# The diagonal and the first neighbour level of a gated recurrence: matrix products before, elementwise products summed over rows by four wide matrix products after

## The chip, the cores and the metric

The kernel runs on one core of one Trainium2 chip. The metric is the device time of one execution in microseconds (us). TensorE (PE in the profile) multiplies matrices: it holds one 128x128 operand (its load is PEld) and streams the other, up to 512 columns, past it. VectorE (DVE), ScalarE (ACT) and GpSimd (POOL) do elementwise work, and SyncE (SP) issues transfers. Each engine takes its own instructions in a fixed order. An instruction that waits for another engine holds everything behind it on its own engine.

## The reference, cut to what matters

The kernel computes one layer of an encoder on 512 tokens of width 1024: attention beside a bidirectional gated recurrence, then attention into a memory, then a gated MLP. The change concerns the recurrence:

```python
def step(S, xs):
    qx, kx, vx, lx = xs
    bcum = jnp.cumsum(lx, axis=-2)
    diff = bcum[..., :, None, :] - bcum[..., None, :, :]
    dec = jnp.exp(jnp.where(tri, diff, -jnp.inf))
    a = jnp.einsum("...tk,...sk,...tsk->...ts", qx, kx, dec)
    o_intra = jnp.einsum("...ts,...sv->...tv", a, vx)
    ...
out = out[0] + flip(out[1])
```

For each of 4 heads this is an attention without softmax. The weight between positions t and s is a sum over 128 key channels of q at t, k at s and the product of the gates between them; k is one minus the gate. It runs forward and backward, and both results are added. So the diagonal (s = t) gets q times the sum of both k, and the pair of positions 2i and 2i+1 gets q times k times one gate.

## The kernel before, in words

Channels lie on the 128 partitions and the 512 tokens along a row. Most of the program is fp32 arithmetic from parts: each operand is split into a rounded part `hi` (type fp32r) and a rest `lo`, and `mm3` (lines 277 to 280) multiplies hi with hi, hi with lo and lo with hi. These wide products (128x512) are nearly all of TensorE's rows.

The recurrence is `hgrn_core(h)`, one call per head. It works by levels m = 1, 2, 4 to 256. At level m, q and k have been multiplied by the gates up to the edge of their block of m positions. A 128x128 product per block of 128 tokens then gives the weights between neighbouring blocks of m, and a mask picks them into `diag`. One level goes so: ScalarE copies the k side of level m into `kc` (line 644), TensorE multiplies four 128x128 blocks (line 647), VectorE multiplies the k side and then the q side by the gates of the next level (line 673, two instructions), multiplies pairs of gates (line 678) and puts the result into `diag` by mask (line 679). Ahead of that, `ksum` is the sum of both directions' k (lines 628 and 629), `kc` and `qc` are gathered (line 632), the product of `ksum` with `q` (line 636) gives the diagonal, and ScalarE copies it into `diag` (line 637). Level 1 uses `kc` and `qc`. These products take plain fp32 operands, in which the trace shows two records per 128x128 product.

`weave` interleaves streams of work. Three heads of the core run between the input projections (share 53 of 100), the fourth beside the attention. Each `yield` of a stream says how much was done. The framework then gives each engine a fixed order, by what it reckons to be ready. `mem_turn` (lines 803 to 806) transposes the memory rows (line 317) into the PSUM banks `ps_s` and `ps_o`, from which lines 121 and 122 split them on ScalarE and VectorE; each bank name has two buffers, and the next token projection (`put`s into `ps_s` and `ps_o`) needs them back. At the end of a head, ScalarE squares the output (line 691), GpSimd takes the power (lines 296 and 297), VectorE scales (line 697) and TensorE transposes (line 701). `put_f` (lines 603 to 607) makes the gates and gated q of a head.

Of the kernel before, what the change touches and what calls it, by code (L numbers as in the profile page):

```python
# [9 lines left out]
F32 = mybir.dt.float32  # L10
F32R = mybir.dt.float32r
BF16 = mybir.dt.bfloat16
U8 = mybir.dt.uint8
# [36 lines left out]
CORE_SHARE, ATT_LEAD = 53.0, 4.0  # L50
KEY_TURNS = {1: (0, 1), 2: (2, 3)}
# [38 lines left out]
def layer(tc, io, out):  # L90
# [17 lines left out]
    def bank(tag):  # L108
        return ps.tile([P, 512], F32, name="ps_" + tag, tag=tag)
# [172 lines left out]
    def blk(b):  # L282
        return slice(b * P, (b + 1) * P)
# [156 lines left out]
    ones = const.tile([P, P], F32, name="ones")  # L440
# [97 lines left out]
    masks = const.tile([P, len(LEVELS), P], U8, name="masks")  # L538
    masks_f = tmp4([P, len(LEVELS), P])
# [4 lines left out]
    with tc.issue_after(last_load[0]):  # L544
        nc.sync.dma_start(lbt, io["hg_lb"])
        nc.sync.dma_start(og, io["hg_out_norm_g"][:, None])
        nc.sync.dma_start(masks_f, io["masks"])
# [70 lines left out]
    def hgrn_core(h):  # L618
# [8 lines left out]
        ksum, kc, qc = [tmp2(tag="th") for _ in range(3)]  # L627
        nc.scalar.mul(ksum, qk[:, 1, 0, :], oml[:, 0, h:h + 1])
        nc.vector.scalar_tensor_tensor(out=ksum, in0=qk[:, 1, 1, :], scalar=oml[:, 1, h:h + 1], in1=ksum,
                                       op0=ALU.mult, op1=ALU.add)  # L630
        for side, to in ((1, kc), (0, qc)):
            (nc.vector.tensor_copy if (h, side) == (1, 0) else nc.scalar.copy)(
                to, pat(qk, side * 2 * T, [[2, T // 2], [T + 1, 2]]))
        o = bank("c").rearrange("p (b n) -> p b n", b=NB)
        for b in range(NB):
            nc.tensor.matmul(o[:, b, :], ksum[:, blk(b)], q[:, blk(b)], start=True, stop=True)
        nc.scalar.copy(diag, o)
        yield 1.0
        toff = 0
        for i, m in enumerate(LEVELS + (128, 256)):  # L640
            if m <= 64:
                if m > 1:
                    kc = tmp2(tag="th")
                    nc.scalar.copy(kc, pat(qk, 2 * T, [[2 * m, T // (2 * m)], [T + m, 2], [1, m]]))
                o = bank("c").rearrange("p (b n) -> p b n", b=NB)
                for b in range(NB):
                    nc.tensor.matmul(o[:, b, :], kc[:, blk(b)], qc[:, blk(b)] if m == 1 else  # L647
                                     pat(qk, b * P, [[2 * m, P // (2 * m)], [T + m, 2], [1, m]]),
                                     start=True, stop=True)
# [6 lines left out]
            else:  # L656
# [18 lines left out]
            if m < 128:  # L675
                src = tt[:, toff:toff + 2 * nblk].rearrange("p (i two) -> p two i", two=2)
                toff += 2 * nblk
                nc.vector.tensor_mul(tt[:, toff:toff + nblk], src[:, 0, :], src[:, 1, :])
                nc.vector.copy_predicated(diag, masks[:, i:i + 1, :].to_broadcast([P, NB, P]), o)
            else:  # L680
                nc.scalar.copy(a[:, :, 1, :], o)
            yield 1.0
# [664 lines left out]
```

## Time and profile before

| | |
|---|---|
| three timed runs | 815.26, 815.65, 817.07 us |
| median | 815.65 us |
| span of the profiled execution, first to last instruction | 813.8 us |
| what lies around the span, against the median | 1.85 us |
| granted TensorE clock, mean | 0.998 |
| heads 0 to 3 of the recurrence in the trace, first product of line 636 | 54.3, 99.5, 130.8, 195.4 us |

| stretch, us | PE busy | DVE busy | ACT busy |
|---|---|---|---|
| 50 to 76 (head 0) | 26.00 of 26 | 18.37 | 15.18 |
| 100 to 124 (head 1) | 23.28 of 24 | 19.73 | 12.83 |
| 124 to 160 (memory rows, head 2) | 35.92 of 36 | 24.97 | 21.84 |
| 160 to 194 (rotary queries) | 34.00 of 34 | 24.35 | 23.94 |
| 194 to 212 (keys, start of head 3) | 17.34 of 18 | 15.57 | 16.37 |

Busy time of TensorE is reckoned from modelled ends, so the trace's starts say more: the time from one start to the next is what a product costs the stream. In a row of the timeline the first number is the start, the second the busy time, both in us, then the engine, the line of the program, the operation, what it writes and reads, and how many instructions are merged. A bracket gives the idle time just before, and who ended it.

### The profile page before, as it was taken

What the parts mean: (1) busy time and instruction counts of PE and PEld (TensorE: products, weight loads), DVE (VectorE), ACT (ScalarE), POOL (GpSimd) and SP (SyncE); (2) the same over time, 40 slices, a digit from 0 to 9 for tenths busy, and PEclk for the clock granted to TensorE, in tenths of its full rate; (3) what the DMA queues carried; (4) which work ended last, traced back from release to release, by engine and by line L of the source; (5) the groups of instructions that cost most, each with busy time, mean ns of one, the idle gap of its engine ahead of it and who ended that gap; (6) DMA issues with size and microseconds to landing.
All of it is one profiled execution on the core that took longest, in us unless ns stands there. A gap on an engine that the chain in (4) does not pass through costs nothing.

```text
span 813.8 us, 11771 instructions
## 1 busy us (share of the span) xinstructions
PE 803.3 (99%) x4426; PEld 691.0 (85%) x4426; DVE 574.7 (71%) x868; ACT 482.1 (59%) x796; POOL 136.9 (17%) x213
## 2 busy tenths in 40 slices
PE   9999999999999999999999999999999999999996
PEld 7888888889998887888888898899999998888885
DVE  5456587469886865855453767987777788888765
ACT  5675757459988874644543553665555545566651
POOL 0111201053233102301010311211111111000301
PEclk9999999999999999999999999999999999999999
DMA  8685645569899753256634158776665677278852
GB/s 296 202 259 139 160 103 117 118 159 247 229 250 254 182 172 126 78 181 157 180 117 142 33 164 208 154 200 166 179 171 143 150 200 178 91 208 278 239 130 104
DMA packets 42457, 139.61 MB, mean 172 GB/s; under 512 B 5280, under 2 KB 6560, under 8 KB 42400
## 3 DMA queue, kind: packets, MB, share of 16 engines
q1 hardware_dynamic: 28944, 97.43, 35.5%
q0 software_dynamic: 12160, 38.54, 26.2%
q10 hardware_dynamic: 1296, 2.89, 1.0%
q8 instruction: 34, 0.56, 0.3%
q14 instruction: 23, 0.19, 0.1%
HBM read 135.17 MB, written 25.17 MB: 197 GB/s over the span
## 4 chain that ended last, share of the span: by engine, by line
PE 92%; DVE 3%; ACT 2%; issue 1%; POOL 1%; DMA 0%; DVEq 0%; POOLq 0%; SPq 0%; ACTq 0%
PE ps_b L279 10%; PE ps_b L280 10%; PE ps_b L278 10%; PE ps_s L278 6%; PE ps_s L280 6%; PE ps_s L279 6%; PE ps_o L278 5%; PE ps_o L279 5%; PE ps_o L280 5%; PE ps_c L278 5%; PE ps_c L280 5%; PE ps_c L279 5%; PE ps_c L647 3%; PE ps_o L893 2%; PE ps_s L872 2%; PE ps_o L882 2%
## 5 line engine op out<-in xcount | busy, mean ns | idle before, releaser
L222 ACT CAST wh<-raw 128x1024 fp32r<-128x1024 f32 x110 | 113.7, 1035 | 114.6 <-PE ps_b L279 35.3
L224 DVE TENSOR_TENSOR wl<-raw,wh 128x1024 fp32r<-128x1024 f32 (+1 forms) x77 | 92.3, 1201 | 72.2 <-ACT wh L222 72.0
L278 PE MATMUL ps_b<-big,wh 128*128 128x512 f32 (+1 forms) x344 | 122.3, 355 | 0.0
L280 PE MATMUL ps_b<-big,wl 128*128 128x512 f32 (+1 forms) x344 | 121.2, 352 | 0.0
L279 PE MATMUL ps_b<-big,wh 128*128 128x512 f32 (+1 forms) x344 | 121.2, 352 | 0.0
L280 PEld LDWEIGHTS ps_b<-big,wl 128*128 128x128 f32 x344 | 65.1, 189 | 8.5 <-DMA wl<-in_wu_dram 0.2
L278 PEld LDWEIGHTS ps_b<-big,wh 128*128 128x128 f32 x344 | 65.1, 189 | 8.3
L279 PEld LDWEIGHTS ps_b<-big,wh 128*128 128x128 f32 x344 | 65.1, 189 | 8.1
L673 DVE TENSOR_TENSOR big<-big 128x512 f32<-128x512 f32 x64 | 47.2, 755 | 9.6 <-PE ps_c L647 4.0
L278 PE MATMUL ps_s<-wh,big 128*128 128x512 f32 (+1 forms) x140 | 53.4, 383 | 0.0
L279 PE MATMUL ps_s<-wl,big 128*128 128x512 f32 (+1 forms) x140 | 53.3, 381 | 0.0
L280 PE MATMUL ps_s<-wh,big 128*128 128x512 f32 (+1 forms) x140 | 53.0, 379 | 0.0
L230 POOL DMA_DIRECT2D wl<-in_w_dram x33 | 29.3, 887 | 126.7 <-ACT wl L229 91.5
L122 DVE TENSOR_TENSOR big<-ps_o,big 128x512 fp32r<-128x512 f32 x54 | 36.9, 687 | 15.0 <-ACT big L121 13.4
L121 ACT CAST big<-ps_o 128x512 fp32r<-128x512 f32 x54 | 31.7, 588 | 18.5 <-PE ps_o L996 7.5
L278 PE MATMUL ps_s<-big,wh 128*128 128x256 f32 (+1 forms) x120 | 40.0, 334 | 0.0
L279 PE MATMUL ps_s<-big,wh 128*128 128x256 f32 (+1 forms) x120 | 40.0, 333 | 0.0
L280 PE MATMUL ps_s<-big,wl 128*128 128x256 f32 (+1 forms) x120 | 40.0, 333 | 0.0
L278 PE MATMUL ps_o<-wh,big 128*128 128x512 f32 (+1 forms) x102 | 39.2, 385 | 0.0
L279 PE MATMUL ps_c<-big,wh 128*128 128x256 f32 (+1 forms) x120 | 39.1, 326 | 0.0
L278 PE MATMUL ps_c<-big,wh 128*128 128x256 f32 (+1 forms) x120 | 39.1, 326 | 0.0
L280 PE MATMUL ps_c<-big,wl 128*128 128x256 f32 (+1 forms) x120 | 39.1, 326 | 0.0
(315 smaller groups left out, 2149.3 us busy)
## 6 DMA issues: line engine op xcount, KB each, us to landing
raw<-in_w_dram SPq DMA_DIRECT2D x91, 512.0 KB, 3.6
wl<-in_w_dram POOLq DMA_DIRECT2D x33, 512.0 KB, 7.3
sum_t<-in_wd_dram SPq DMA_DIRECT2D x20, 512.0 KB, 6.3
tmp<-in_wu_dram SPq DMA_DIRECT2D x14, 512.0 KB, 6.9
sum_t<-in_wd_dram POOLq DMA_DIRECT2D x10, 512.0 KB, 8.4
sum_t<-sum_t POOLq DMA_DIRECT2D x10, 512.0 KB, 7.5
big<-sum_t SPq DMA_DIRECT2D x10, 512.0 KB, 4.7
raw<-sum_t SPq DMA_DIRECT2D x10, 512.0 KB, 4.4
```

The costliest lines, as they stand in the source:

```text
L121: nc.scalar.copy(hi, src)
L122: (eng or nc.vector).tensor_sub(lo, src, hi.bitcast(F32))
L222: nc.scalar.copy(wh, raw)
L224: last_low[0] = nc.vector.tensor_sub(wl[:, :by_dma], raw[:, :by_dma], wh[:, :by_dma].bitcast(F32)).ins
L230: nc.gpsimd.dma_start(wl[:, by_dma:], source(i)[:, by_dma:], accum_op=ALU.add)
L278: nc.tensor.matmul(o, a[0], b[0], start=start, stop=False, skip_group_check=again)
L279: nc.tensor.matmul(o, a[0], b[1], start=False, stop=False, skip_group_check=again)
L280: last_mm[0] = nc.tensor.matmul(o, a[1], b[0], start=False, stop=stop, skip_group_check=again).ins
L647: nc.tensor.matmul(o[:, b, :], kc[:, blk(b)], qc[:, blk(b)] if m == 1 else pat(qk, b * P, [[2 * m, P // (2 * m)], [T + m, 2], [1, m]]), st ...
L673: nc.vector.tensor_tensor(out=c, in0=c, in1=pat(tt, toff + off, [[2, npair], [gap, 2], [0, m]]), op=ALU.mult)
L872: nc.tensor.matmul(s, qT[h // 4][:, h % 4, blk(qb)], kT[:, 2 * (h // 4) + c, :], start=c == 0, stop=c == 1)
L882: nc.tensor.transpose(o[:, c, :], e[:, 0, blk(c)], ident)
```

## The change

The diagonal and level 1 no longer go through 128x128 products of their own. VectorE forms the elementwise products of q and k for the diagonal and for the neighbouring position, in two instructions, into a tile `near` with two rows of 512: the first row holds, for each t, the term of the even s of t's pair, the second that of the odd s. ScalarE and VectorE split `near` into `hi` and `lo` (128x1024 each). TensorE sums over the 128 channels by multiplying with `parity`, a constant of alternating ones and zeros: with it shifted by one column for the second row, even output rows take the first row and odd ones the second. That is four 128x512 products per head. ScalarE copies the result into `diag`, whose other entries the masks of the later levels overwrite. The gather of `kc` and `qc` for level 1, its products and its mask are gone; the mask tile has 6 levels in place of 7. A `yield` of 1.5 (`PREP`) stands between the split and the four products, and the yield of 1.0 for level 1 is gone. `ones` moves from a constant to a temporary.

```diff
+PREP = 1.5
-    ones = const.tile([P, P], F32, name="ones")
+    parity = const.tile([P, P + 2], F32R, name="parity")
+    ones = tmp2((P, P), tag="tq")
     nc.gpsimd.memset(ones, 1.0)
+    for i in range(2):
+        nc.gpsimd.memset(parity.rearrange("p (i two) -> p i two", two=2)[:, :, i].bitcast(F32), 1.0 - i)
...
-        ksum, kc, qc = [tmp2(tag="th") for _ in range(3)]
+        near = room[:, 1024:2048]
+        ksum = tmp2(tag="th")
         nc.scalar.mul(ksum, qk[:, 1, 0, :], oml[:, 0, h:h + 1])
+        nc.vector.tensor_tensor(out=pat(near, T, [[2, T // 2], [1 - T, 2]]), in0=pat(qk, 0, [[2, T // 2], [T + 1, 2]]),
+                                in1=pat(qk, 3 * T + 1, [[2, T // 2], [-(T + 1), 2]]), op=ALU.mult)
         nc.vector.scalar_tensor_tensor(out=ksum, in0=qk[:, 1, 1, :], scalar=oml[:, 1, h:h + 1], in1=ksum,
                                        op0=ALU.mult, op1=ALU.add)
-        for side, to in ((1, kc), (0, qc)):
-            (nc.vector.tensor_copy if (h, side) == (1, 0) else nc.scalar.copy)(
-                to, pat(qk, side * 2 * T, [[2, T // 2], [T + 1, 2]]))
-        o = bank("c").rearrange("p (b n) -> p b n", b=NB)
-        for b in range(NB):
-            nc.tensor.matmul(o[:, b, :], ksum[:, blk(b)], q[:, blk(b)], start=True, stop=True)
-        nc.scalar.copy(diag, o)
+        pairs = lambda t: t.rearrange("p (i two) -> p i two", two=2)
+        nc.vector.tensor_tensor(out=pat(near, 0, [[2, T // 2], [T + 1, 2]]), in0=pairs(ksum), in1=pairs(q), op=ALU.mult)
+        hi, lo = [tmp4([P, 2, T], F32R) for _ in range(2)]
+        split(hi, lo, near.rearrange("p (a t) -> p a t", a=2))
+        yield PREP
+        o = bank("c")
+        for i in range(2):
+            for part in (hi, lo):
+                nc.tensor.matmul(o, parity[:, i:i + P], part[:, i], start=i == 0 and part is hi, stop=i == 1 and part is lo)
+        nc.scalar.copy(diag, o.rearrange("p (b n) -> p b n", b=NB))
         yield 1.0
...
-            if m <= 64:
-                if m > 1:
-                    kc = tmp2(tag="th")
-                    nc.scalar.copy(kc, pat(qk, 2 * T, [[2 * m, T // (2 * m)], [T + m, 2], [1, m]]))
+            if 1 < m <= 64:
+                kc = tmp2(tag="th")
+                nc.scalar.copy(kc, pat(qk, 2 * T, [[2 * m, T // (2 * m)], [T + m, 2], [1, m]]))
...
-                nc.vector.copy_predicated(diag, masks[:, i:i + 1, :].to_broadcast([P, NB, P]), o)
+                if m > 1:
+                    nc.vector.copy_predicated(diag, masks[:, i - 1:i, :].to_broadcast([P, NB, P]), o)
...
-            yield 1.0
+            if m > 1:
+                yield 1.0
```

The framework orders the engines anew. Three places matter below. Line numbers of the changed kernel are larger: its 278 to 280 are 279 to 281, 121 and 122 are 122 and 123, 126 is 127, 317 is 318, 577 is 581, 607 is 611, 647 is 656, 673 is 682, 678 is 687, 697 is 708, 701 is 712.

**TensorE in head 1, before.** In these rows `tmp2_733` is q, `tmp2_892` is `ksum`, and `ps_b_877` and `ps_b_1002` are two projections of head 2 of 24 wide products each.

```order
L278 MATMUL ps_b_877<-big_114,wh_737 128x512
L636 MATMUL ps_c_899<-tmp2_733,tmp2_892 128x128 x4
L279 MATMUL ps_b_877<-big_116,wh_737 128x512
L280 MATMUL ps_b_877<-big_114,wl_738 128x512
L278 MATMUL ps_b_877<-big_114,wh_737 128x512
L647 MATMUL ps_c_905<-tmp2_894,tmp2_893 128x128 x4
L279 MATMUL ps_b_877<-big_116,wh_737 128x512
L647 MATMUL ps_c_916<-big_731,tmp2_914 128x128 x4
L280 MATMUL ps_b_877<-big_114,wl_738 128x512
```

TensorE in head 1, after. `ps_b_876` and `ps_b_986` are the same two projections; `tmp4_896` is `hi`, `tmp4_897` is `lo`, and line 656 is level 2.

```order
L280 MATMUL ps_b_986<-big_118,wh_772 128x512
L281 MATMUL ps_b_986<-big_116,wl_773 128x512
L646 MATMUL ps_c_900<-tmp4_896,parity_86 128x512
L279 MATMUL ps_b_986<-big_116,wh_772 128x512
L656 MATMUL ps_c_911<-big_708,tmp2_909 128x128 x4
L646 MATMUL ps_c_900<-tmp4_897,parity_86 128x512
L646 MATMUL ps_c_900<-tmp4_896,parity_86 128x512
L646 MATMUL ps_c_900<-tmp4_897,parity_86 128x512
L280 MATMUL ps_b_986<-big_118,wh_772 128x512
```

The core's first product moved from within the first projection (13 wide products of it done) to the tenth place of the second (24 and 9 done). Level 2 now stands between the first and the second of the four summing products.

**TensorE where the memory rows are turned, before.** Ahead of these rows stand the last product of head 1's line 687 and 11 of 14 wide products of `ps_b_1082`. Line 317 turns the memory rows, line 701 the output of head 1 (`tmp2_1073`), and `ps_s_1163` is the first bank of the next token projection.

```order
L278 MATMUL ps_b_1082<-big_114,wh_823 128x512
L279 MATMUL ps_b_1082<-big_116,wh_823 128x512
L280 MATMUL ps_b_1082<-big_114,wl_824 128x512
L317 MATMUL ps_s_1122<-ident_84,big_454 128x128 x4
L317 MATMUL ps_o_1129<-ident_84,big_454 128x128 x4
L317 MATMUL ps_s_1136<-ident_84,big_454 128x128 x4
L317 MATMUL ps_o_1143<-ident_84,big_454 128x128 x4
L701 MATMUL ps_c_1184<-ident_84,tmp2_1073 128x128 x3
L278 MATMUL ps_s_1163<-wh_880,big_113 128x512
```

TensorE there, after. Line 698 is the old 687, 712 the old 701, and `ps_s_1158` is the first bank of the token projection.

```order
L697 MATMUL ps_c_1075<-big_325,big_890 128x128
L698 MATMUL ps_c_1075<-big_890,big_708 128x128
L281 MATMUL ps_b_1055<-big_117,wl_823 128x512
L318 MATMUL ps_s_1117<-ident_84,big_457 128x128 x4
L318 MATMUL ps_o_1124<-ident_84,big_457 128x128 x4
L318 MATMUL ps_s_1131<-ident_84,big_457 128x128 x4
L318 MATMUL ps_o_1138<-ident_84,big_457 128x128 x4
L712 MATMUL ps_c_1185<-ident_84,tmp2_1088 128x128 x4
L279 MATMUL ps_s_1158<-wh_879,big_116 128x512
```

Between the last product of head 1's core and the turning of the memory rows stood 14 wide products; now one does. The other 13 run earlier, between the levels of head 1.

**VectorE at the same place, after.** `tmp2_1109` is the last projection of head 2, line 708 the scaling of head 1's output, line 611 head 2's gated q, line 123 the rest of the split that gives `ps_s` and `ps_o` back.

```order
L581 TENSOR_TENSOR tmp2_1109<-ps_b_1055,big_301 128x512
L708 SCALAR_TENSOR_TENSOR tmp2_1088<-ps_c_1075,small_1094,big_657 128x128 x4
L611 SCALAR_TENSOR_TENSOR big_873<-big_874,oml_316,tmp2_875 128x512
L123 TENSOR_TENSOR big_1116<-ps_s_1117,big_1115 128x4x128
L123 TENSOR_TENSOR big_1116<-ps_o_1124,big_1115 128x4x128
```

VectorE there, before: `tmp2_1073` is the output of head 1, and line 122 gives `ps_s_1122` back.

```order
L697 SCALAR_TENSOR_TENSOR tmp2_1073<-ps_c_1060,small_1079,big_666 128x128 x4
L577 TENSOR_TENSOR tmp2_1114<-ps_b_1082,big_298 128x512
L122 TENSOR_TENSOR big_1121<-ps_s_1122,big_1120 128x4x128
L629 SCALAR_TENSOR_TENSOR tmp2_1192<-big_874,oml_313,tmp2_1192 128x512
L607 SCALAR_TENSOR_TENSOR big_874<-big_875,oml_313,tmp2_876 128x512
```

The release of the first `ps_s` bank now stands behind head 2's gated q (line 611) as well as behind the scaling of head 1.

More of the change, by code (lines that the diff above doesn't have):

```diff
@@ L536, in spread_r @@
             put_v(b, v_ps[b])
-    masks = const.tile([P, len(LEVELS), P], U8, name="masks")
-    masks_f = tmp4([P, len(LEVELS), P])
+    masks = const.tile([P, len(LEVELS) - 1, P], U8, name="masks")
+    masks_f = tmp4([P, len(LEVELS) - 1, P])
     lbt = const.tile([P, 2, 2, 4], F32, name="lbt")
@@ L546, in layer @@
         nc.sync.dma_start(og, io["hg_out_norm_g"][:, None])
-        nc.sync.dma_start(masks_f, io["masks"])
+        nc.sync.dma_start(masks_f, io["masks"][:, 1:, :])
         nc.sync.dma_start(qkg[:, 0, :], rows_bc(io["q_norm_g"], 64))
@@ L655, in hgrn_core @@
                                      start=True, stop=True)
-            else:
+            elif m == 256:
                 o = bank("c").rearrange("p (b n) -> p b n", b=NB)
```

2 lines of the change are left out of this document (1 added, 1 removed).

## The prediction

> **What bounds the kernel now.** I read the page's busy times first, then its chain of work that ended last, then TensorE's timeline in the four stretches in which a head of the recurrence runs.
>
> ```profile
> span 813.8 us, 11771 instructions
> PE 803.3 (99%) x4426; PEld 691.0 (85%) x4426; DVE 574.7 (71%) x868; ACT 482.1 (59%) x796; POOL 136.9 (17%) x213
> PE 92%; DVE 3%; ACT 2%; issue 1%; POOL 1%; DMA 0%; DVEq 0%; POOLq 0%; SPq 0%; ACTq 0%
> ```
>
> TensorE is busy for 803.3 of 813.8 us and makes 92% of the chain. So a product taken out of its stream is worth its whole length, and a wait put into it costs its whole length: its order is fixed, nothing overtakes. The median of the runs, 815.65 us, lies 1.85 above the span; I take those 1.85 as unchanged and reckon differences in the span.
>
> **What the products cost TensorE.** From the timeline of TensorE, head 0, and the groups by line:
>
> ```profile
> 54.08 0.39 PE L280 MATMUL ps_o<-wh,big 128*128 128x512 f32 x1
> 54.31 1.05 PE L636 MATMUL ps_c<-tmp,tmp 128*128 128x128 f32 x8
> 55.11 0.48 PE L278 MATMUL ps_o<-wh,big 128*128 128x512 f32 x1
> 55.43 1.05 PE L647 MATMUL ps_c<-tmp,tmp 128*128 128x128 f32 x8
> 56.24 0.48 PE L279 MATMUL ps_o<-wl,big 128*128 128x512 f32 x1
> ...
> 91.76 0.39 PE L278 MATMUL ps_b<-big,wh 128*128 128x512 f32 x1
> 99.24 0.39 PE L278 MATMUL ps_b<-big,wh 128*128 128x512 f32 x1
> ...
> L636 PE MATMUL ps_c<-tmp,tmp x32: 271/276/351, 54.3 to 196.2; 128*128 128x128 f32 x32
> L647 PE MATMUL ps_c<-tmp,tmp x32: 271/275/377, 55.4 to 200.0; 128*128 128x128 f32 x32
> ```
>
> Between 91.76 and 99.24 lie 33 wide products (7.48 us): 0.227 each. From 54.31 to 55.43 a group of line 636 and one wide product take 1.12, so the group costs 0.89, the slower start of the product behind it included. Removed are the groups of line 636 and of line 647 on `tmp`, 32 records each, 8 to a group: 8 groups, 7.12 us. Added are 16 wide products: 3.63 us. The trace has no row of a product with `parity`; its operands are fp32r like those of `mm3`, so I take 0.227. Bounds: 0.22 (the 0.89 of a plain fp32 group, spread over its 4 products) and 0.89 (plain fp32 over 512 columns). **Gain of TensorE's stream: 3.5 us**, 0.87 per head. It is the whole gain only if the new products find their operands ready.
>
> **Head 1: the longer way to the first product.** The chain here is VectorE's:
>
> ```profile
> 100.01 0.68 DVE L678 TENSOR_TENSOR big<-big 128x512 f32<-128x512 f32 x1
> 100.61 0.50 DVE L632 COPY tmp<-big 128x512 f32<-128x512 f32 x1
> 101.04 2.15 DVE L673 TENSOR_TENSOR big<-big 128x512 f32<-128x512 f32 x2
> 103.04 0.40 DVE L678 TENSOR_TENSOR big<-big 128x256 f32<-128x256 f32 x1
> 103.37 0.71 DVE L679 COPY_PREDICATED big<-masks,ps_c 128x512 f32<-128x512 uint8 x1
> 103.98 1.29 DVE L673 TENSOR_TENSOR big<-big 128x512 f32<-128x512 f32 x2
> ...
> 102.14 0.47 PE L279 MATMUL ps_b<-big,wh 128*128 128x512 f32 x1
> 103.33 1.20 PE L647 MATMUL ps_c<-big,tmp 128*128 128x128 f32 x8 [0.72 <-DVE big L673]
> ...
> L222 ACT CAST wh<-raw 128x1024 fp32r<-128x1024 f32 x110 | 113.7, 1035 | 114.6 <-PE ps_b L279 35.3
> L224 DVE TENSOR_TENSOR wl<-raw,wh 128x1024 fp32r<-128x1024 f32 (+1 forms) x77 | 92.3, 1201 | 72.2 <-ACT wh L222 72.0
> ```
>
> Level 2 came 1.19 after the wide product ahead of it, where 0.23 would do: a wait of 0.96, because line 673 at level 1 takes 1.0 for each side (101.04 to 103.04), at level 2 about 0.6. The two products into `near` (lines 634 and 639 of the changed kernel) are not in this trace. Line 634 reads and writes in the pattern of level 1: 1.0. Line 639 reads straight and writes in that pattern: 0.6 to 1.0; I take 0.8, the middle of its two nearest rows. hi is a cast of 128x1024 (1.0), lo a subtraction of that size (1.2).
>
> The Trainium skill, SBUF — State Buffer, section "Door 1: The DMA port swizzle", says that accesses keep full bandwidth when at least two in a row hit the same 16-byte line, and pay otherwise. The rows 101.04 and 103.98 agree (single elements 1.0, pairs 0.6). By that rule line 639, which writes single elements, would take 1.0, and the sum below would be some 0.4 us later.
>
> By the new order, on the clock of this trace: gate pairs until 100.61, line 634 until 101.6, gate pairs 0.33, line 639 until 102.7, two sides of level 1 until 104.7, gate pairs and a projection's line 581 until 105.5, lo until 106.7. ScalarE casts hi from 102.9 to 103.9, after a weight cast that waits for the end of the projection. TensorE comes to hi after 21 wide products from 99.24, at 104.0: no wait. Level 2 (104.5) waits for its q side until 104.8, and lo, 0.89 later, from 105.7 to 106.7. Together 1.3, with line 639 at its ends 1.1 to 1.5, for the 0.96 and some 0.1 at the group ahead of it that go: **+0.2, bounds 0 to +0.5**. In head 0 the same order leaves nine wide products (2 us) more before hi, and I find no wait.
>
> **Where the memory rows are turned.** Here the moved work counts. TensorE, ScalarE and VectorE before:
>
> ```profile
> 123.58 0.48 PE L279 MATMUL ps_b<-big,wh 128*128 128x512 f32 x1
> 126.88 0.60 PE L317 MATMUL ps_s<-ident,big 128*128 128x128 f32 x4
> 128.63 0.49 PE L701 MATMUL ps_c<-ident,tmp 128*128 128x128 f32 x3
> 129.16 0.50 PE L278 MATMUL ps_s<-wh,big 128*128 128x512 f32 x1
> ...
> 123.86 0.28 ACT L691 ACTIVATE tmp<-ps_c 128x128 f32<-128x128 f32 x1 [1.42 <-PE ps_c L687]
> 128.28 0.63 ACT L603 ACTIVATE big<-tmp 128x512 f32<-128x512 f32 x1
> 130.04 0.57 ACT L121 CAST big<-ps_o 128x512 fp32r<-128x512 f32 x1
> ...
> 126.44 1.13 DVE L697 SCALAR_TENSOR_TENSOR tmp<-ps_c,small,big 128x128 f32<-128x128 f32 x4 [3.21 <-POOL small L297]
> 127.49 0.68 DVE L577 TENSOR_TENSOR tmp<-ps_b,big 128x512 f32<-128x512 f32 x1
> 128.42 0.69 DVE L122 TENSOR_TENSOR big<-ps_s,big 128x512 fp32r<-128x512 f32 x1 [0.25 <-ACT big L121]
> 130.18 0.75 DVE L607 SCALAR_TENSOR_TENSOR big<-big,oml,tmp 128x512 f32<-128x512 f32 x1
> ```
>
> Let X be 123.58, when head 1's last product has left TensorE. ScalarE's squares, GpSimd's power and VectorE's scaling (line 697) take until X + 3.9. Before, 14 wide products and the turning covered that; the token projection at 129.16 started when line 122 had freed `ps_s`, 0.3 late. After, one wide product is left there. TensorE has that (0.31), the turning (126.88 to 128.63, 1.75) and four transposes (0.44): 2.5. `ps_s` comes free later: VectorE scales until X + 3.9, then does line 611 (0.7, for which ScalarE's lines 607 to 609 are ready in time: 1.76 as from 128.28 to 130.04, begun at about X + 1.3), then line 123 (0.7): X + 5.3. TensorE stands 2.8 for 0.3: **+2.5**. Bounds: 1.8 if line 611 cost nothing; 2.9 if the transposes, too, came only after the release.
>
> **Head 2.** The same queue leads on to head 2's `near`:
>
> ```profile
> 132.04 0.68 DVE L122 TENSOR_TENSOR big<-ps_o,big 128x512 fp32r<-128x512 f32 x1
> 132.79 0.43 DVE L715 TENSOR_TENSOR big<-big,qkg 128x256 f32<-128x256 f32 x1
> 134.14 0.69 DVE L678 TENSOR_TENSOR big<-big 128x512 f32<-128x512 f32 x1
> 134.74 0.75 DVE L126 SCALAR_TENSOR_TENSOR big<-ps_c,og,big 128x512 fp32r<-128x512 f32 x1
> 135.40 2.15 DVE L673 TENSOR_TENSOR big<-big 128x512 f32<-128x512 f32 x2
> ```
>
> From X + 5.2: three more splits (1.8), four rotary tables (1.35, from 132.79 to 134.14), line 634 (1.0), line 127 (0.66), `ksum` (0.66), one side (1.0), line 639 (0.8): X + 12.5. The cast makes hi at X + 13.5. TensorE reaches it 34 wide products after X + 5.3: X + 13.0, a wait of 0.5. lo is ready at X + 15.3 (one side 1.0, gates 0.6, lo 1.2), TensorE there at X + 14.6: 0.7. Together 1.2 for some 0.3 spread over head 2 before: **+0.9, bounds 0.5 to 1.2**.
>
> **Head 3** starts in the stretch of keys and attention. Before, level 2 waited there for ScalarE:
>
> ```profile
> 207.46 1.16 PE L647 MATMUL ps_c<-big,tmp 128*128 128x128 f32 x8 [0.52 <-ACT tmp L644]
> ```
>
> After, lo has to wait behind the first three keys in VectorE's order, and level 2 stands behind more projection work. That wait may go, stay, or be one like head 1's: **-0.2, bounds -0.5 to +1.0**. GpSimd's two fills of `parity` and SyncE's smaller mask transfer lie beside the first loads. VectorE's added work per head (1.0 + 0.8 + 1.2, less 0.6 for one mask) costs nothing where VectorE idles; if that cover were gone it would be 2.4 per head.
>
> **Sum.** -3.5 + 0.2 + 2.5 + 0.9 - 0.2 = -0.1, so 815.55: **815.5 us**. The change takes out what it says, and nearly all of it stands again as waits for VectorE. The terms' bounds add up to 814.0 and 817.8.
>
> **The rivals.** (a) *The waits are covered.* If the hole at the memory rows does not open (its work runs earlier than my walk has it), 2.5 comes back: 813.0. For it speaks that the chain before shows VectorE with only 3%; against it that the bank's release stands behind line 611 in the order. If head 1 and 2 run freely as well, 3.5 and the old 0.96 are gained: 811.2. (b) *VectorE bounds the start of the attention: slower.* In head 3, `near` and lo stand ahead of the last key in VectorE's queue. If the last key comes later than TensorE's turn of it, the attention starts late by up to the added 2.4, and with the upper ends of heads 1 and 2 (+0.6) it is 815.5 + 3.0 = 818.5. It decides from the point at which what is given back passes 3.5. Against it: level 1's two sides (2.0) moved behind the keys. (c) *The summing products do not run at 0.227* but at twice that, as two passes: 16 x 0.227 = 3.6 more, 819.1; at plain fp32's 0.89, 16 x 0.66 = 10.6 more, 826. Against it stand all rows of fp32r.
>
> **How the numbers follow.** A measurement of this kernel can tell about 0.2% (1.6 us) from no change: 814.0 to 817.3 is "same". My forecast's own range is 814.0 to 817.3, inside its bounds; it has 0.48. (a) has 0.32, all faster. (b) has 0.17 and (c) 0.03, all slower. The range for 8 in 10 reaches to 812.2 below, past (a)'s first value and to 818.0 above, past the sum of the upper bounds, to the lower half of (b).
>
> **What would show it.** In the changed profile: 16 products on `parity` at 0.23 from start to start; in head 1 a wait of about 1 ahead of the second of them, for VectorE's lo; TensorE idle for 2 to 3 us ahead of the first token projection into `ps_s`, ended by VectorE's line 123; in head 2 about half a microsecond ahead of the first and of the second summing product. The prediction is wrong if that idle time is under 1 us, or if the keys' transposes in head 3 wait for over 1 us.

## The result, and the profile after

| | before | after |
|---|---|---|
| median of the timed runs, us | 815.84 | 818.49 |
| runs, us | 815.26 to 817.30 | 817.48 to 821.37 |
| ratio of after to before, 95% interval | | 1.0033, 1.0023 to 1.0044 |
| span of the profiled execution, us | 813.8 | 816.8 |

The change made the kernel 0.33% slower; 815.5 had been forecast, and the range ended at 818.0. Of the experiments below, one execution of PREP 1.0 (1136 us) and one of PREP 1.0 with the seeds later (963 us) ran at granted clocks of 0.66 and 0.78: the ratios leave them out, the medians without them are 814.24 and 814.88 us, and the second was the profiled one, so its waits are left blank. On the page of the changed kernel, the span, the busy times and the chain of work that ended last:

```profile
span 816.8 us, 11680 instructions
PE 802.4 (98%) x4378; PEld 687.1 (84%) x4378; DVE 583.4 (71%) x875; ACT 481.7 (59%) x793; POOL 137.2 (17%) x215
...
PE 88%; DVE 6%; ACT 2%; DMA 2%; issue 1%; POOL 0%; DVEq 0%; POOLq 0%; SPq 0%
```

TensorE's share of the chain fell from 92 to 88%. VectorE has 6 for 3, and the DMAs, which had none, have 2. So TensorE waits more. Where, its timeline shows; a bracket holds the idle time ahead of the row and who ended it:

```profile
104.82 1.20 PE L656 MATMUL ps_c<-big,tmp 128*128 128x128 f32 x8 [0.31 <-DVE big L687]
106.57 0.97 PE L646 MATMUL ps_c<-tmp,parity 128*128 128x512 f32 x3 [0.55 <-DVE tmp L123]
129.30 1.01 PE L712 MATMUL ps_c<-ident,tmp 128*128 128x128 f32 x4 [1.14 <-DVE tmp L708]
131.24 0.50 PE L279 MATMUL ps_s<-wh,big 128*128 128x512 f32 x1 [0.93 <-DVE big L123]
139.73 0.50 PE L646 MATMUL ps_c<-tmp,parity 128*128 128x512 f32 x1 [0.49 <-ACT tmp L122]
...
181.30 0.85 PE L791 MATMUL ps_c<-ident_r,tmp 128*128 128x128 f32 x8 [0.61 <-DVE tmp L123]
...
205.34 0.50 PE L646 MATMUL ps_c<-tmp,parity 128*128 128x512 f32 x1 [0.46 <-ACT tmp L122]
210.67 1.20 PE L656 MATMUL ps_c<-big,tmp 128*128 128x128 f32 x8 [0.55 <-DVE big L687]
214.09 1.16 PE L656 MATMUL ps_c<-big,tmp 128*128 128x128 f32 x8 [0.33 <-ACT tmp L653]
```

Line 646 multiplies with `parity`, 656 is a level's product, 712 transposes a head's output, 279 starts a wide product, 791 turns the rotary queries. For sums over the whole span I took every pair of neighbouring products and counted as waiting what lies from one start to the next beyond 0.228 us (512 columns), 0.118 (256) or 0.111 (128), the usual steps. Such a wait is a little longer than the bracket, since the product behind it starts slowly. The rows of the single stretches list waits of 0.15 us or more; the sums take every pair, so "all else" holds the many small ones.

| where TensorE waits, us | before | after | difference | forecast |
|---|---|---|---|---|
| first 12 us | 3.34 | 4.03 | +0.69 | 0 |
| head 1 | 0.96 | 1.36 | +0.40 | +0.2 |
| memory rows | 0.21 | 2.74 | +2.53 | +2.5 |
| head 2 | 0.20 | 0.98 | +0.78 | +0.9 |
| rotary queries | 0 | 0.77 | +0.77 | no term |
| keys and head 3, 203 to 215 us | 0.98 | 2.00 | +1.02 | -0.2 |
| all else | 6.7 | 6.9 | +0.2 | 0 |
| sum | 12.4 | 18.8 | +6.4 | |

6.4 us of new waits less the 3.5 us that were taken out of the stream are 2.9; the span grew by 3.0. The signs that the prediction had named are there, in size or nearly: the 16 products at 0.23, head 1's wait ahead of the second of them (0.72 for about 1), the hole that line 123 ends, the two waits in head 2. What it missed stands elsewhere: in head 3's products and levels, at the rotary queries and in the first 12 us.

### The profile page after: what moved, and what is told of

The parts are those of the page before. It is cut to its first block, busy times and chain, and to the rows that moved or that the text cites. A ratio compares the mean times of both kernels' runs of the same rounds, so it can differ in the third digit from the quotient of the medians.

```text
span 816.8 us, 11680 instructions
## 1 busy us (share of the span) xinstructions
PE 802.4 (98%) x4378; PEld 687.1 (84%) x4378; DVE 583.4 (71%) x875; ACT 481.7 (59%) x793; POOL 137.2 (17%) x215
## 4 chain that ended last, share of the span: by engine, by line
PE 88%; DVE 6%; ACT 2%; DMA 2%; issue 1%; POOL 0%; DVEq 0%; POOLq 0%; SPq 0%
PE ps_b L280 9%; PE ps_b L281 9%; PE ps_b L279 9%; PE ps_s L281 6%; PE ps_s L280 6%; PE ps_s L279 6%; PE ps_o L279 5%; PE ps_o L281 5%; PE ps_o L280 5%; PE ps_c L279 5%; PE ps_c L280 5%; PE ps_c L281 5%; PE ps_c L656 3%; PE ps_o L904 2%; DMA raw<-in_w_dram 2%; PE ps_s L883 2%
```

## The experiments

Each kernel ran beside the kernel before on the same chip; a ratio is to that kernel. Of the waits, those of the table above are meant. Lines of an experiment's kernel are up to ten off those of the changed one.

### Work or place?

Two explanations stood against each other: the added elementwise work is too slow, or the core now stands at a worse place among the wide products. **No near**: lines 633 to 639 go, and the split reads other rows.

```diff
-        split(hi, lo, near.rearrange("p (a t) -> p a t", a=2))
+        split(hi, lo, qk[:, 0])
```

> The changed kernel without VectorE's and ScalarE's new preparation: lines 633 to 639 (key sums and both near products) are left out, and the split into hi and lo reads the gated queries instead, so the diagonal and neighbour level hold other numbers. The wide products, their place in TensorE's order and the later place of the core stay. Theory A (the saved time is given back because the core now stands later among the wide products: the hole at the memory rows and the wait at the rotary queries): those two stay at 2.5 to 3.0 and 0.5 to 0.8 us, the waits ahead of hi in heads 1 to 3 fall by 1 to 2 us in all, so 816.0 to 817.5. Theory B (the added elementwise work is too slow wherever it stands): 812 to 813.5, both waits gone. Theory C (the wide products cost more than what they replace): 818 or more.

**Before, later second core**, with no new work at all:

```diff
                 nc.scalar.copy(kt, o)
-                yield 0.5
+                yield 3.0 if h == 1 else 0.5
```

> The kernel before with no new work at all: only the second core's yield after its key transposes is 3.0 instead of 0.5, so that its last products stand 2 wide products ahead of the memory rows' transposes instead of 15, as in the changed kernel (2). Theory A: a hole of 2.3 to 2.9 us opens there, with some tenths more where the third core, now 4 us later, meets the rotary queries: 818.0 to 819.0 against 815.8, and nothing else in the trace changes. Theory B: within 0.5 us of before.

**PREP 1.0** and **PREP 0**:

```diff
-PREP = 1.5
+PREP = 1.0
```

> The changed kernel with PREP 1.0 instead of 1.5: same instructions, the core stands some 2 wide products nearer; the first block of memory rows is then turned ahead of the second core's last products and the second behind 4 us of wide products. Theory A: the hole of 2.75 us shrinks to under 1.0, the third core's normalisation and the rotary queries no longer meet, heads 1 to 3 wait as long or 0.3 us longer each: 815.0 to 816.8. Theory B: within 0.6 us of the changed kernel, 818 to 819.

```diff
-PREP = 1.5
+PREP = 0.0
```

> The changed kernel with PREP 0: the summing products are asked for right behind the split, and the third core ends 8 us earlier among the wide products. Theory A: no hole at the memory rows (under 1.0 us), no wait at the rotary queries (under 0.2), against 0.3 to 0.8 us more in each of heads 1 to 3 ahead of hi: 815.5 to 818.0. Theory B: as slow as the changed kernel or slower by what the missing cover costs, 818 to 820.

| | median, us | ratio to before | head 1 | memory rows | head 2 | rotary | 199 to 215 us |
|---|---|---|---|---|---|---|---|
| changed kernel | 818.49 | 1.0033 (1.0023 to 1.0044) | 1.36 | 2.74 | 0.98 | 0.77 | 2.00 |
| no near | 814.25 | 0.9982 (0.9972 to 0.9991) | 0.62 | 1.46 | 0 | 0.78 | 1.23 |
| before, later second core | 817.55 | 1.0023 (1.0012 to 1.0034) | 0.95 | 2.06 | 0 | 0 | 0.52 |
| PREP 1.0 | 814.35 | 0.9981 (0.9971 to 0.9991) | 1.36 | 0.83 | 0 | 0 | 1.63 |
| PREP 0 | 815.84 | 0.9996 (0.9987 to 1.0005) | 1.38 | 1.97 | 0.37 | 0 | 1.06 |

Neither explanation holds alone. The same instructions in the order that PREP 1.0 gives run 4.1 us faster, faster even than before; theory B had excluded that, and A had it less far. The second core doesn't stand nearer there, as had been expected: in both traces its first summing product comes behind 373 wide products (two of 256 columns counted as one), and its last product comes behind 412 with PREP 1.0, behind 411 without. What moved is the first turning of the memory rows, now ahead of the core's last products, and the end of the third core, 12 wide products earlier. Without the near products, at the old PREP, 4.2 us go as well, where A had 1 to 2.5. That isn't the price of the work alone, since the framework moved this order too: the second core's first summing product comes behind 361 wide products. And the kernel before, with none of the new work, gets 0.23% slower from the order alone. Of the 2.6 us by which the span of its profiled execution grew, 1.9 stand at the memory rows (and 1.55 at the attention's scores at 218.7 us, against savings elsewhere). Its TensorE at the memory rows:

```profile
130.39 0.30 PE L701 MATMUL ps_c<-ident,tmp 128*128 128x128 f32 x1 [1.50 <-DVE tmp L697]
130.90 0.50 PE L278 MATMUL ps_s<-wh,big 128*128 128x512 f32 x1 [0.21 <-DVE big L122]
```

The transposes of the normalised output (line 701) wait for VectorE's scaling, as in the changed kernel. By these runs, what costs is late work on VectorE at a place where nothing covers it; take away either, and most of it goes. The rotary wait needs no near products (0.78 without them), and goes with PREP 1.0 and 0, where the third core ends earlier: it is the place. Head 1's wait is the work: no PREP moves it, and without the near products it is 0.62. With PREP 0, another 1.97 us stand at the memory rows, before the transposes of the output; theory A's "under 1.0" missed that.

With PREP 1.0 the first block of memory rows is transposed from 121.59 us, ahead of the second core's last products. TensorE's one wait there, and the kernel's chain:

```profile
129.32 0.50 PE L279 MATMUL ps_o<-wh,big 128*128 128x512 f32 x1 [0.67 <-DVE big L123]
...
PE 93%; DVE 4%; ACT 1%; issue 0%; DMA 0%; POOL 0%; DVEq 0%; POOLq 0%; SPq 0%
```

### What makes the hole at the memory rows

The changed kernel's row at 129.30 names VectorE's scaling. **Memory first** puts the scaling behind the memory splits; the other three of the group keep that order.

```diff
+        with tc.issue_after(mem_last[0]) if h == 1 else ExitStack():
             for b in range(NB):
                 nc.vector.scalar_tensor_tensor(out=on[:, b, :], in0=o[:, b, :], scalar=r[:, b:b + 1],
```

> The changed kernel (PREP 1.5) with one order fixed on VectorE: the second core's scaling (line 708) is issued behind the four splits of the turned memory rows, instead of ahead of them. Nothing else is edited. Theory D (VectorE's queue is in order: the scaling stands at its head, waits 1.66 us for GpSimd, and holds back the memory splits, and behind them the third core's near products): the hole of 2.74 us falls to under 1.0, and the wait of 0.98 us ahead of the third core's summing products to under 0.3, the one of 0.77 at the rotary queries stays: 815.2 to 816.4 against 818.5. Rival E (the hole is only the outward sign; what VectorE has to do is too much there): the wait moves to the scaling's transposes or the next head, and the time stays over 817.5.

With the edit of no near on top of it:

> The kernel of the run before with lines 633 to 639 left out (as in the first run; the summed values are then others). This prices the elementwise work where its order is mended. Theory D1 (the work is covered once the order is mended, but for head 1 and head 3): 1.0 to 2.0 us less than the run before, 813.5 to 815.0. Theory D2 (the work costs as much as with the old order, where leaving it out gave 4.2 us): 811 to 812.5. Theory D3 (it is covered altogether): within 0.6 us of the run before.

With the near products written contiguously, and the wide products reading every second column:

```diff
-        out=pat(near, T, [[2, T // 2], [1 - T, 2]])
+        out=pairs(near[:, T:])
-        out=pat(near, 0, [[2, T // 2], [T + 1, 2]])
+        out=pairs(near[:, :T])
-        nc.tensor.matmul(o, parity[:, i:i + P], part[:, i], ...
+        nc.tensor.matmul(o, parity[:, i:i + P], pat(part, i * T, [[2, T // 2], [T + 1 - 2 * i * T, 2]]), ...
```

> The kernel of the first run of this group, with the two near products written one behind the other in full rows, and the reading of every second column given to the wide products' moving operand (step of 2 elements, then half a row on). Line 639 then reads and writes full rows: 0.60 to 0.68 us apart instead of 0.95 if scattered elements are its price, 0.95 if not; line 634 still gathers its operands and stays near 0.95. If TensorE reads the gathered operand at the pace of a full row (0.23 us), the head's chain is 0.35 us shorter and the time 0.3 to 0.8 us less; if it reads it at half the pace, 16 products cost 0.23 each more, and the time is 3 us more.

With lines 634 to 639 of head 3 issued behind the last key:

```diff
+        with tc.issue_after(key_last[0]) if h == 3 else ExitStack():
```

> The kernel of the first run of this group, with head 3's near products and key sum (lines 634 to 639) issued on VectorE behind the last rotated key (line 761). Theory F (head 3's waits come from sharing VectorE with the keys' chain): the key transposes' wait (0.23) goes and the last key is some 3 us earlier, the summing products come 3 us later and wait as before or less, 0.5 to 1.2 us less in time. Rival G (the products then come so late that the levels behind them meet the softmax): the wait moves to the levels, same time or up to 1 us more.

| | median, us | ratio to before | head 1 | memory rows | head 2 | rotary | 199 to 215 us |
|---|---|---|---|---|---|---|---|
| memory first | 819.31 | 1.0044 (1.0027 to 1.0061) | 1.37 | 2.54 | 0.86 | 0.77 | 1.81 |
| and no near | 812.73 | 0.9962 (0.9947 to 0.9977) | 0.64 | 0.38 | 0 | 0.77 | 0.96 |
| and contiguous | 819.91 | 1.0044 (1.0028 to 1.0060) | 0.91 | 2.54 | 0.46 | 0.77 | 1.81 |
| and keys first | 822.11 | 1.0075 (1.0060 to 1.0090) | 1.39 | 2.54 | 0.84 | 0.77 | 4.45 |

Theory D fell: the scaling is out of the way, and the hole is as long. In memory first, ScalarE, VectorE and TensorE at the hole:

```profile
127.12 0.65 ACT L608 ACTIVATE big<-tmp 128x512 f32<-128x512 f32 x1
128.16 0.82 ACT L610 ACTIVATE big<-big,lb,oml 128x512 f32<-128x512 f32 x1
128.87 0.59 ACT L122 CAST big<-ps_s 128x512 fp32r<-128x512 f32 x1
...
129.02 0.75 DVE L612 SCALAR_TENSOR_TENSOR big<-big,oml,tmp 128x512 f32<-128x512 f32 x1 [1.99 <-ACT big L610]
129.69 0.68 DVE L123 TENSOR_TENSOR big<-ps_s,big 128x512 fp32r<-128x512 f32 x1
...
130.43 0.50 PE L280 MATMUL ps_s<-wh,big 128*128 128x512 f32 x1 [2.38 <-DVE big L123]
```

The rows of lines 608 to 612 are the gate of head 2 (607 to 611 in the changed kernel). They stand ahead of the first memory split on both engines: hi is made at 128.87, lo at 129.69, and only then is `ps_s` free. In the kernel before, the first hi stood ahead of the gate, which the prediction's rows show from 128.28 on:

```profile
127.81 0.58 ACT L121 CAST big<-ps_s 128x512 fp32r<-128x512 f32 x1
```

So two chains of nearly the same length end in this hole, the second core's scaling and the third head's gate, and mending one shows the other. That also spoils the price that the second run of this group was to give: without the near products the framework put the first hi ahead of the gate again, and the 6.6 us between that run and memory first are work and order together.

Writing the near products contiguously did to VectorE what was expected. In that run lines 640 (639 before), 636 (634) and the next:

```profile
99.51 0.69 DVE L640 TENSOR_TENSOR big<-tmp,tmp 128x512 f32<-128x512 f32 x1
100.11 0.84 DVE L636 TENSOR_TENSOR big<-big 128x512 f32<-128x512 f32 x1
100.87 0.68 DVE L688 TENSOR_TENSOR big<-big 128x512 f32<-128x512 f32 x1
```

They are 0.60 and 0.76 us long from start to start, where the changed kernel has for line 639

```profile
203.01 1.12 DVE L639 TENSOR_TENSOR big<-tmp,tmp 128x512 f32<-128x512 f32 x1
203.96 0.42 DVE L761 TENSOR_TENSOR big<-tmp,big 128x256 fp32r<-128x256 f32 x1
```

0.95. TensorE gathers every second column at no price: in the groups by line, the 16 products come to the same mean of 431 ns in the changed kernel and in this one:

```profile
L646 PE MATMUL ps_c<-tmp,parity 128*128 128x512 f32 x16 | 5.6, 431 | 1.7 <-ACT tmp L122 1.0 <-DVE tmp L123 0.7
```

```profile
L647 PE MATMUL ps_c<-tmp,parity 128*128 128x512 f32 x16 | 5.6, 431 | 0.9 <-ACT tmp L122 0.5 <-DVE tmp L123 0.2
```

Head 1's wait fell by 0.46 us and head 2's by 0.40. But the time didn't fall: the profiled execution has 0.6 us more in the first 12 us, and 1.4 more behind the memory rows, where seven wide products start 0.43 us apart instead of 0.23. That is TensorE's clock and not the edit's order. Of these rows the last one is a sum over 131 to 134 us; behind the busy time and count of each engine it gives the granted clock, 0.54, then the DMA share and GB/s:

```profile
131.04 0.63 PE L281 MATMUL ps_s<-wl,big 128*128 128x512 f32 x1
131.47 0.63 PE L282 MATMUL ps_s<-wh,big 128*128 128x512 f32 x1
...
131.00:134.00 3.00, 3.00 (x9) 2.34 (x8) 3.00 (x10) 1.91 (x4) 0.92 (x1) 0.54 0.01 3
```

Two other traces have such a drop between 12 and 800 us: keys first (0.50 from 208 to 214 us) and first split ahead of the next group (0.54 from 215 to 218). Each begins within about 1 us of the end of a TensorE wait of over 2.3 us. The traces of all the runs have six waits of that length; three were followed by a drop and three were not (in memory first, in memory early and the first of the two in keys first), and no other trace at full clock has a drop there. By the starts of its products, TensorE lost 1.6 to 2.7 us in each drop, on top of the wait. Why one wait brings it and another doesn't stays open, and so does whether the contiguous writing saves time by itself.

Keys first was a miss for both theories: TensorE waited less for head 3's products, but 2.57 us for VectorE's split of a projection. VectorE waited in its turn for ScalarE's hi, which stood behind a weight cast that waited 2.00 us for its load:

```profile
205.66 1.05 ACT L225 CAST wh<-raw 128x1024 fp32r<-128x1024 f32 x1 [2.00 <-DMA raw<-in_w_dram]
...
208.56 0.58 PE L281 MATMUL ps_b<-big,wh 128*128 128x256 f32 x1 [2.57 <-DVE big L123]
```

### The hole mended, and no time gained

**First split ahead**, on top of memory first: when head 2's last projection is done, the first block of memory rows is turned and split, and only then `put_f(1)` makes the gate.

```diff
+            if ahead:
+                ahead()
             scaled(put_f(1))(o)
```

> The changed kernel with the scaling behind the memory splits (as in memory-first, where the hole stayed at 2.54 us), and now also the first block of memory rows turned and split ahead of the last gate of the third head on ScalarE and VectorE (lines 607 to 611), as it stood before the change. Theory H (the hole is the gate's chain: VectorE's 581, ScalarE's three activations, VectorE's 611, 3.3 us, all ahead of the first memory split, which the first token projection waits for): the hole falls from 2.54 to 0.4 to 0.9 us, and the time by 1.6 to 2.2 against memory-first (819.3), if the gate that is now later isn't missed; head 2's summing products wait 0.5 to 1.0 longer if it is. Rival I (the hole is the ScalarE squares and GpSimd's power of the second core): hole stays over 2 us, same time.

**Memory early**: both blocks are turned behind head 2's second projection.

```diff
             yield from proj_fm(hT, T, "b", scaled(put))
+            if ahead and i == 1:
+                for b in range(MB):
+                    ahead(b)
```

> The changed kernel (PREP 1.5) with the memory rows turned one projection earlier, 8 us of wide products ahead of the last gate; nothing else edited. Theory H: no hole is left where they are turned (under 0.4 us), the rotary queries' wait (0.77) and the waits of heads 1 and 3 (1.4 and 2.0) stay: 815.2 to 816.4 against 818.5. Rival J (VectorE and ScalarE are full there: the four splits, 1.1 us each on the two engines, delay head 1's levels): 1 us or more appears in head 1's levels, 817 or more.

Memory early with contiguous near products and PREP 1.0:

> Memory rows turned early as in the run before, PREP 1.0, and the near products written contiguously (line 639 0.60 us apart instead of 0.95, line 634 0.76 instead of 0.98; 16 summing products at the same 0.23). Theory H with the place of the core: no hole (0.83 in the run with PREP 1.0), no rotary wait, head 1 0.9 instead of 1.36: 812.6 to 814.0, faster than before by 0.2 to 0.4%. Rival J: 815 or more.

Memory early in the kernel before:

> The kernel before, with only the memory rows turned one projection earlier: a control. Theory H: before had a hole of 0.21 us there, so at most 0.4 us is gained, 815.3 to 816.2. If it gains 1 us or more, the early turning is worth something by itself and says nothing of the change.

| | median, us | ratio to before | head 1 | memory rows | head 2 | rotary | 199 to 216 us |
|---|---|---|---|---|---|---|---|
| first split ahead | 818.21 | 1.0025 (1.0012 to 1.0039) | 1.36 | 0.61 | 0.55 | 0.79 | 4.58 |
| memory early | 818.90 | 1.0030 (1.0019 to 1.0042) | 1.36 | 0 | 2.18 | 0.78 | 4.04 |
| early, contiguous, PREP 1.0 | 814.76 | 0.9982 (0.9972 to 0.9991) | 0.90 | 1.19 | 0.58 | 0 | 1.93 |
| before, memory early | 816.33 | 1.0000 (0.9991 to 1.0009) | 0.96 | 0 | 0.87 | 0 | 0.98 |

Theory H on the hole is shown: with the first split ahead of the gate, the hole is 0.61 us for 2.54. In first split ahead:

```profile
126.62 0.60 ACT L122 CAST big<-ps_s 128x512 fp32r<-128x512 f32 x1
...
127.57 0.68 ACT L608 ACTIVATE big<-tmp 128x512 f32<-128x512 f32 x1
...
128.01 0.50 PE L280 MATMUL ps_s<-wh,big 128*128 128x512 f32 x1 [0.45 <-DVE big L123]
```

But the times that H gave are not: both mended kernels stay where the changed kernel is. In memory early, head 2 waits 1.2 us more, 1.45 of its 2.18 ahead of hi, which is cast later; head 1, where rival J had its price, waits as before. The kernel before gains nothing by turning early, as its control had it. The version with contiguous products and PREP 1.0 is above H's 814.0, and 1.19 us stay at its memory rows, where H had none. In first split ahead and memory early, a wait of 2.6 us stands at 213 to 215 us, where the changed kernel had 0.49. Level 4's copy of k sits on ScalarE behind the cast of a weight block, and the cast waits for its load. Memory early, ScalarE, and below it the load and the seed issued with it (KB each, us from issue to landing):

```profile
213.75 1.04 ACT L223 CAST wh<-raw 128x1024 fp32r<-128x1024 f32 x1 [3.35 <-DMA raw<-in_w_dram]
```

```profile
raw<-in_w_dram SPq DMA_DIRECT2D x1, 512.0 KB, 12.0
sum_t<-in_wd_dram SPq DMA_DIRECT2D x1, 512.0 KB, 15.4
```

The load took 12.0 us. Issued at the same place, it took 6.7 in the kernel before and 9.9 in the changed one:

```profile
raw<-in_w_dram SPq DMA_DIRECT2D x1, 512.0 KB, 6.7
```

```profile
raw<-in_w_dram SPq DMA_DIRECT2D x1, 512.0 KB, 9.9
```

These are the weight casts ahead of it, first of the kernel before, then of the changed kernel:

```profile
184.61 1.04 ACT L222 CAST wh<-raw 128x1024 fp32r<-128x1024 f32 x1
190.49 1.03 ACT L222 CAST wh<-raw 128x1024 fp32r<-128x1024 f32 x1
196.42 1.05 ACT L222 CAST wh<-raw 128x1024 fp32r<-128x1024 f32 x1
```

```profile
185.97 1.05 ACT L223 CAST wh<-raw 128x1024 fp32r<-128x1024 f32 x1
194.87 1.04 ACT L223 CAST wh<-raw 128x1024 fp32r<-128x1024 f32 x1
198.51 1.04 ACT L223 CAST wh<-raw 128x1024 fp32r<-128x1024 f32 x1
...
212.47 1.05 ACT L223 CAST wh<-raw 128x1024 fp32r<-128x1024 f32 x1 [1.28 <-DMA raw<-in_w_dram]
```

A cast frees the buffer for the next load. Two more transfers of 512 KB follow each: a seed, the load that starts a sum of weights (`sum_t`), and an accumulate, with which GpSimd adds a weight block onto the negated hi in `wl` so that the rest is left. Before, these casts come 5.9 us apart. After, the second comes 8.9 us behind the first: ScalarE has the gate of head 3 ahead of it, and the gate's input (line 581) leaves VectorE only at 192.4. The loads behind it are then issued 3 to 4 us apart, and each takes longer than the one before, 3.3, 6.1 and 9.9 us. The last group takes the seeds out of this stretch.

```diff
-SEEDS_AT = frozenset(range(28, 46)) | frozenset(range(60, 66))
+SEEDS_AT = frozenset(range(34, 52)) | frozenset(range(60, 66))
```

> Memory rows turned early (PREP 1.5), and the first 18 seeds of the weight sums (512 KB loads each) start at weight unit 34 instead of 28, so none shares the DMA engines in the stretch from 185 to 215 us. Theory K (the load that ScalarE waits for at 214 us, 12 us from issue to landing, is late because the DMA engines are full): it lands in under 7 us, the wait of 2.59 us falls to under 0.7, and the time by 1.5 to 2.5, to 816.4 to 817.4. Rival L (the levels stand in the wrong place whatever the load does): wait stays over 1.5 us, 818 to 819.

> The changed kernel with the seeds six units later, nothing else. Theory K: of its own waits only the 0.49 us at 214 us (ScalarE 1.28 us idle for the load) hangs on the DMA: 0.3 to 0.8 us less than 818.5. Rival L: 818.2 to 818.9.

> The kernel before with the seeds six units later: control. No wait for a load stands in its trace there, so both theories: within 0.6 us of 815.9. More than 1 us less would mean that the seeds cost before the change too.

> The changed kernel with PREP 1.0 and the seeds six units later. With PREP 1.0 ScalarE waited 0.38 us for that load and two levels 0.48 and 0.20: theory K 0.2 to 0.7 us less than the 814.35 of PREP 1.0; rival L the same time. Both below before.

| with the seeds later | median, us | ratio to before | 199 to 215 us |
|---|---|---|---|
| memory early | 816.88 | 1.0012 (1.0002 to 1.0021) | 1.47 |
| changed kernel | 817.92 | 1.0026 (1.0016 to 1.0037) | 1.47 |
| before | 816.66 | 1.0010 (1.0001 to 1.0020) | 0.97 |
| PREP 1.0 | 815.09 | 0.9989 (0.9979 to 0.9998) | |

Theory K holds. In memory early with the seeds later, the load issued at the same place and the cast that had waited:

```profile
raw<-in_w_dram SPq DMA_DIRECT2D x1, 512.0 KB, 7.6
```

```profile
209.01 1.07 ACT L223 CAST wh<-raw 128x1024 fp32r<-128x1024 f32 x1
```

7.6 us for 12.0 (not quite the 7 expected), no wait for the cast, the 2.59 us gone, and the median 2.0 us lower than memory early's. In the changed kernel the 0.49 us went; its time can't be told from what it was. The remedy has a price of its own: the kernel before got 0.1% slower, with a wait of 1.06 us at 351 us, and the changed kernel with the seeds later has 1.46 at 352 to 353. For PREP 1.0 it was no gain. Shown is that the load is late because other transfers share the engines; that the late cast bunches them is read from the two traces and wasn't tested by itself.

By these traces, TensorE reaches this stretch earlier by what it saves further ahead, and waits there for transfers. It is no fixed floor: with PREP 1.0 the load at that place took 9.5 us, and its cast waited only 0.38. In the two runs without near products TensorE waited there for an accumulate; memory first, no near:

```profile
206.36 0.39 PE L282 MATMUL ps_b<-big,wl 128*128 128x256 f32 x1 [0.80 <-DMA wl<-in_w_dram]
```

## Why the prediction was wrong, point by point

- **TensorE's stream, -3.5: right.** The 16 products on `parity` stand 0.23 us apart, 0.33 where a wait precedes, as the trace's rows of `mm3` let expect. New waits of 6.4 us less the span's 3.0 leave 3.4 saved. Rival (c) is out.
- **Head 1, +0.2: 0.40,** inside the bounds. Line 639 was taken at 0.8 and took 0.95, as the rule of the Trainium skill, SBUF — State Buffer, section "Door 1: The DMA port swizzle", has it for single elements, in the sentence that was kept out of the sum. The trace agrees, for scattered writing too: contiguous, the line takes 0.60. Of the 0.20 missed that would be 0.15.
- **Memory rows, +2.5: 2.53.** Size and place are right, and so is the walk along line 708, line 611 and line 123. What the walk didn't have is that on ScalarE the first memory hi now stands behind the gate, so that the gate's chain ends nearly as late as the scaling's: with the scaling out of the way, the hole stayed at 2.54.
- **Head 2, +0.9: 0.78,** 0.66 ahead of hi and 0.32 ahead of lo, less the 0.2 of before, for 0.5 and 0.7 expected: the sum came out nearer than its parts, which is partly luck.
- **Head 3, -0.2: 1.02. This step failed.** "That wait may go, stay, or be one like head 1's": it put a small gain for what it couldn't walk, and the wait measured lies at the upper bound of +1.0. The summing products, the key transposes and two levels wait, 0.59, 0.23, 0.69 and 0.49. Without the near products none of these stands, but 1.23 us for an accumulate; so lines 633 to 639 cost some 0.8 net here, as far as an order that moved with them can tell. The 0.49 is a load's, and went with the seeds: whether the weight stream would shift was nowhere asked.
- **Rotary queries: no term, 0.77. This was left out.** The prediction stopped at head 2's start and took its end as unmoved. Its end stands later, and by the trace VectorE's scaling of head 2's output (172.85 to 176.88 us) falls among the rotary work, which TensorE waits for at 181.30. PREP 1.0 undoes it.
- **First 12 us: no term, +0.69.** It can't be laid to the change: over the runs the waits of this stretch lie between 2.9 and 4.0 with the new start, and between 3.3 and 3.9 with the old one. What differs in these two traces is TensorE's pace: in the changed one the first wide products start 0.43 us apart from 5.87 to 7.15 us, the pace of the clock's drop above (though the profile shows no lower clock here), in the one before 0.23 from 5.86 on.

Head 3, the rotary queries and the first 12 us are 1.22, 0.77 and 0.69 of the 3.1 us by which the sum missed. Rival (b), 818.5, had the time and not the mechanism: the key transposes wait 0.23 us, well under its "over 1 us", and head 3 gives 1.0 of its 3.0. What it had right is that near and lo stand among the keys. Rival (a), 813.0, is nearly what the change does with PREP 1.0: 814.35, 0.19% (0.09 to 0.29) below before. That version, and the one with memory early, contiguous and PREP 1.0 (814.76), are faster than both kernels; the two can't be told apart.

Two things stay open: the price of lines 633 to 639 at an order that doesn't move when they go, and whether the rotary wait can be mended by itself, which wasn't tried.

## What to carry to other kernels

When TensorE sets the time and every engine keeps a fixed order, a saving in its stream is lost or kept by where the work around it lands: walk each stretch behind the moved work to its end, not only the first two. Before a change is given up, its place constant is worth a run or two, since 0.5 in `PREP` was worth more than all the products saved. And where a healed wait doesn't lower the time, look at the next load's landing: casts that an engine's order has pushed together can bring their loads together too. A long wait of TensorE can cost more than its length, since the clock may fall behind it.

## What was not expected of the hardware

A VectorE product of 128x512 with scattered reading and writing (line 634) takes 0.98 us from start to start in head 1, with scattered writing alone (line 639) 0.95, with scattered reading and contiguous writing 0.76, and all contiguous 0.60: the writing is most of the price. TensorE streamed a moving operand of every second column at the same 0.23 us. A 512 KB load took 3.1 us where no other load was issued within 2 us of it (memory early with the seeds later, at 193.88 us), and 12.0 beside seeds and accumulates (memory early). After three of six TensorE waits of over 2.3 us the granted clock stood at about 0.5 for 3 to 7 us, after no shorter one.
